# Recurrence of a hybrid encoder step: units run in pairs of head halves, their outputs placed beside the next pair

## The chip, the cores and the metric

The kernel runs on one core of a Trainium2 chip. Its time is device time in microseconds. It is given as the median of three runs; beside it stands one profiled execution, whose records are the trace that is read here. The engines are PE (TensorE, matrix products, with PEld for its weight loads), DVE (VectorE), ACT (ScalarE), POOL (GpSimd) and the DMA queues, which SP and ACT issue.

## The reference

One inference step of a two-layer encoder for two groups of requests: a prompt of 1024 tokens and eight samples of 16 tokens, 1152 tokens of width 1024. Layer 0 is RWKV-7 time mixing and a SwiGLU feed-forward part; layer 1 is chunk-band attention over one shared K and V, and a second feed-forward part. Both layers are modulated by a condition (shift, scale and gate from `silu(c) @ w_ada`). The part that the change touches is the recurrence of layer 0, over 16 heads of 64:

```python
def step(s, inp):
    r_t, w_t, k_t, v_t, a_t, b_t = inp
    sa = jnp.einsum('bhij,bhj->bhi', s, a_t)
    s = s * w_t[:, :, None, :] + sa[..., None] * b_t[:, :, None, :] + v_t[..., None] * k_t[:, :, None, :]
    y = jnp.einsum('bhij,bhj->bhi', s, r_t)
    return s, y
```

Its output y is normalised per head (mean and variance over 64), scaled, shifted, joined by a bonus term, multiplied by a gate g and projected by `rw_o`. The final states of the prompt and of the samples are outputs too.

## The kernel before

All tensors lie with features on the 128 partitions and tokens along the free dimension. The 1152 tokens are three blocks of 384 (two of the prompt, the third half prompt, half samples). Products are made in three passes over a split of each operand into a high and a low part (`split`, lines 252 to 254), which ACT and DVE make; `mm` (line 138) issues every matrix product, so that products are told apart by their tiles.

**Projections.** `proj(b)` (line 461) makes, for a block, the low-rank parts (`proj_lora`: decay, gate of a, gate g), then `proj_k`, `proj_r`, `proj_v`, each as eight tiles of features. It spills its results to memory in DRAM. The mixed operands are tiles of the tag `mix`, eight high and eight low ones for one projection; the tag has `nmix` = 17 of them. Results on their way to DRAM use tiles of the tag `e0`, four of them, through `ev` (line 453). Beside `proj_r` stand the `inverses(b)` (line 716): for each window of 128 tokens a triangular system is formed (`win_first`), solved in small blocks (`win_solve`) and put together (`win_merge`); the result is the tile TT.

**Windows.** A block has three windows of 128 tokens, and each window two halves `hf` of the heads (four feature tiles, eight heads). A unit is one window and one half. Window 8 is that of the samples. For a unit:

- `win_prep` (728) loads the spilled operands (tiles XL, BK, and UV for v), makes the local matrices by products into the bank tag G (two banks), masks them into XL and YL, and transposes BK into BKT. XL, YL and BKT have three buffers, BK has one, UV two.
- `win_run` (1015) goes through the two chunks of 64 tokens. Each `win_state` (854) has three groups of 16 products: X from UV and XL, copied to `xs` by ACT (line 877); U from `xs` and TT, copied into UV by DVE and ACT (885, 886); the state update from UV and BKT, added and scaled on DVE (910, 912); then `put_state` (940) copies the state into UV for the next chunk (942, 943). All of them use the bank tag `st`, which has two banks; `win_merge` uses it too. For window 8 both chunks run side by side, with more small products (lines 894 to 900).
- `win_y` (918) sums the outputs of a unit in the bank Y, of which there is one. It is called at the end of `win_run`.
- `win_post` (961) loads the gate and bonus (`gl`, `bv`), copies Y into the tile y (line 971, one buffer), normalises it with two products into `st` (971 to 980), applies weights and gate, and stores it to DRAM as `yg` (line 986, on ACT's queue).

The halves of one window don't depend on each other; window w+1 needs the state of window w of the same half.

**Order.** Each part is a generator that yields after a step. `windows(us)` (1031) prepares two units, then runs unit i woven with the output of unit i-1, and prepares one more unit after each run. `alternate(a, b, m, n)` (1004) takes m steps of a and n of b in turn. In `layer0a` (1088) the windows of block b-1 alternate with `proj(b)` at 5 to 4. After the last projections, when the projections' tiles have been released and the pool `tail` has taken their place, the units of windows 6 to 8 alternate at 5 to 2 with `early()`: 32 steps of the modulation (`ada_steps`, weights `in_wada`, loaded into tiles `raw`) and the output projections of blocks 0 and 1 (`outproj`, 1062). `outproj(2)` comes last; it reloads `yg` into tiles `mr` (1070), splits them into `mx` and multiplies. The tail's units are, in this order, (6,0), (6,1), (8,0), (7,0), (7,1), (8,1).

The order in which these generators issue instructions is a priority. A planner simulates the program, and each engine's own order comes from that simulation, by priority among what it takes to be ready. An engine then works through its own list in order, and each queue of DMAs too.

Of the kernel before, what the change touches and what calls it, by code (L numbers as in the profile page):

```python
# [136 lines left out]
def mm(nc, out, lhsT, rhs, start, stop):  # L137
    return nc.tensor.matmul(out, lhsT, rhs, start=start, stop=stop)  # L138


class Trunk:
# [196 lines left out]
    def proj_open(self, ctx):  # L338
        self.pp = ctx.enter_context(self.tc.tile_pool(name="proj", bufs=1, side="right", reuse_waits="tile"))
        self.rawc, self.rawtag = 1024, "raw"  # L340
        self.nraw, self.nhi, self.nlo = 3, 2, 2
        self.nmix, self.nmr = 17, 2
        pp = self.pp
        self.hb = pp.tile([128, 8, 408], F32, name="hb")

# [142 lines left out]
    def proj_r(self, b, hi, lo):  # L488

        nc = self.nc  # L490
        for f in range(8):
            W = self.wunit(self.pp, self.a["rw_r"][f])
            pz = self.bank("acc", 2)
            self.gemm(pz[:, :TB], W, hi, lo)
            kp = self.ev("ag", 2)
            self.load(kp, "kp", b, f)
            ex = self.ev("rr", 2)
            self.load(ex, "cs", b, f)
            nc.scalar.activation(ex, ex, AF.Exp, scale=-KAPPA)
            nc.vector.scalar_tensor_tensor(kp, pz[:, :TB], self.P("rk", f), kp, ALU.mult, ALU.mult)  # L500
            nc.vector.tensor_tensor(ex, ex, pz[:, :TB], ALU.mult)
            self.spill("r", b, f, ex)
            aux = self.bank("aux", 1)
            mm(nc, aux[:, :TB], self.C("bo"), kp, True, True)
            bn = self.ev("e0", 4)
            nc.scalar.activation(bn, aux[:, :TB], AF.Copy)
            self.save("bn", b, f, bn)
            yield

    def proj_lora(self, b, hi, lo):  # L510

        nc, pp = self.nc, self.pp
        split = lambda ts: tuple([self.hgroups(t)[i] for t in ts] for i in range(2))
        (hc, hp), (lc, lp) = split(hi), split(lo)

        def first(n, rows):
            pw = self.bank("acc", 2)
            W = [self.wunit(pp, dt, 8 * rows) for dt in self.lw[n]]
            for i, (h, l) in enumerate(((hc, lc), (hp, lp))):
                for k in range(8):  # L520
                    s = slice(k * rows, (k + 1) * rows)
                    self.mm3(pw[:rows, :TB], W[i][0][:, s], W[i][1][:, s], h[k], l[k], i + k == 0, i + k == 8)
            return pw

        def second(n, t, bias, spill):
            wh, wl = self.wunit(pp, self.a[n])
            for f in range(8):
                fs = slice(f * 128, (f + 1) * 128)
                pz = self.bank("acc", 2)
                mm(nc, pz[:, :TB], wh[:, fs], t, True, False)  # L530
                mm(nc, pz[:, :TB], wl[0:64, fs], t[0:64], False, True)
                sg = self.ev("e0", 4)
                ins = nc.scalar.activation(sg, pz[:, :TB], AF.Sigmoid, bias=self.P(bias, f))
                if spill == "cs":
                    nc.vector.tensor_tensor_scan(sg, rs, sg, 0.0, ALU.mult, ALU.add)
                self.save(spill, b, f, sg)
                if f % 4 == 3:
                    yield
            self.last_sg = ins

        pw = first("wa1", 128)
        yield
        tw, ta = self.ev("ag", 2, F32R), self.ev("ag", 2, F32R)
        th = self.ev("kp")
        nc.scalar.activation(th[:64], pw[:64, :TB], AF.Tanh)
        self.split(tw[0:64], tw[64:128], th[:64])
        th = self.ev("kp")
        nc.scalar.activation(th[:64], pw[64:128, :TB], AF.Copy)
        self.split(ta[0:64], ta[64:128], th[:64])
        pg = first("g1a", 128)  # L550
        yield
        th = self.ev("kp")
        h, l = self.ev("rr", 2, F32R), self.ev("rr", 2, F32R)
        nc.scalar.activation(th, pg[:, :TB], AF.Sigmoid)
        self.split(h, l, th)
        pg = first("g1b", 32)
        yield
        th = self.ev("kp")
        t = self.ev("vv", 2, F32R)
        nc.scalar.activation(th[:32], pg[:32, :TB], AF.Sigmoid)  # L560
        self.split(t[0:32], t[32:64], th[:32])
        nc.scalar.activation(t[64:96], th[:32], AF.Copy)
        rs = self.ev("rs", 1)
        nc.sync.dma_start(rs, self.a["rs"][b // 2])
        yield from second("w2", tw, "w0", "cs")
        yield from second("a2", ta, "a0", "a")
        with self.tc.issue_after(self.last_sg.ins):
            nc.scalar.preload_act_table_set("natural_log_exp_and_others")
        ah, al = self.wunit(pp, self.a["g2a"])
        raw = pp.tile([128, 1024], F32, tag="raw", name=self.nm("raw"), bufs=self.nraw)  # L570
        nc.sync.dma_start(raw[:96], self.a["g2b"])
        bh = pp.tile([128, 1024], F32R, tag="whi", name=self.nm("whi"), bufs=self.nhi)
        nc.scalar.activation(bh[:96], raw[:96], AF.Copy)
        nc.vector.tensor_tensor(bh[64:96], raw[64:96], bh[64:96], ALU.subtract)
        for f in range(8):
            fs = slice(f * 128, (f + 1) * 128)
            pz = self.bank("acc", 2)
            self.mm3(pz[:, :TB], ah[:, fs], al[:, fs], h, l, True, False)
            mm(nc, pz[:, :TB], bh[:96, fs], t[:96], False, True)
            g = self.ev("e0", 4)  # L580
            nc.scalar.activation(g, pz[:, :TB], AF.Copy)
            self.spill("g", b, f, g)
            if f % 4 == 3:
                yield

    def proj_v(self, b, hi, lo):

        nc = self.nc
        for f in range(8):
            W = self.wunit(self.pp, self.a["rw_v"][f])  # L590
            pz = self.bank("acc", 2)
            self.gemm(pz[:, :TB], W, hi, lo)
            if b in (2,):
                self.step(1)
            vv = self.ev("vv", 2)
            self.load(vv, "bn", b, f)
            v = self.ev("e0", 4)
            nc.scalar.activation(v, pz[:, :TB], AF.Copy)
            nc.vector.tensor_tensor(vv, vv, pz[:, :TB], ALU.mult)
            nc.scalar.activation(vv, vv, AF.Identity, bias=self.P("lnb", f))  # L600
            self.spill("v", b, f, vv)
            pt = self.bank("aux", 1)
            for w in range(3):
                nc.tensor.transpose(pt[:, w * 128:(w + 1) * 128], v[:, w * 128:(w + 1) * 128], self.C("ident"))
            vt = self.ev("e0", 4)
            nc.scalar.activation(vt, pt[:, :TB], AF.Copy)
            for e in range(2):
                nc.sync.dma_start(self.sv[b][:, :, e, f, :].rearrange("w p d -> p w d"),
                                  vt.rearrange("p (w e d) -> p e w d", w=3, e=2)[:, e])
            yield  # L610
# [117 lines left out]
    def win_prep(self, w, hf):  # L728

        nc = self.nc  # L730
        smp = w == 8
        b, wi = divmod(w, 3)
        fs = slice(4 * hf, 4 * hf + 4)
        R = Ctx()
# [37 lines left out]
        for e in range(2):  # L772
            nc.scalar.activation(bkt[:, :, e], pt[e].rearrange("p (c f d) -> p c (f d)", c=2, f=4), AF.Copy)
        R.xl, R.yl, R.bkt, R.TT = xl, yl, bkt, self.TT.pop((w, hf))
        uv = R.uv = self.wt("UV", [128, 2, 2, 4, 64], 2)
        for c in range(2):
            for e in range(2):
                p0 = 64 * (1 - e)
# [75 lines left out]
    def win_state(self, w, hf, c, R):  # L854

        nc = self.nc
        TT, xl, uv, bkt = R.TT, R.xl, R.uv, R.bkt
        hs = [slice(0, 64), slice(64, 128)]
        smp = w == 8
        xs = self.wt(f"xs{c if smp else hf}", [128, 4, 64], 1)  # L860
        X = self.bank("st", 2)
        if smp:
            sv = R.sv[c]
# [151 lines left out]
    def win_run(self, w, hf, R):  # L1015
        if w == 8:
            self.win_smp(hf, R)
            gens = [self.win_state(w, hf, c, R) for c in range(2)]
            while gens:
                gens = [g for g in gens if next(g, StopIteration) is not StopIteration]  # L1020
                yield
        else:
# [3 lines left out]
                yield from self.win_state(w, hf, c, R)  # L1026
            if w == 7:
                self.nc.sync.dma_start(self.o["wkv_p"][:, 4 * hf:4 * hf + 4, :], self.S[hf])
        R.Y = self.win_y(w, hf, R)

    def windows(self, us):

        us = list(us)
        n = 2
        r = []
        for u in us[:n]:
            r.append(self.win_prep(*u))
            yield
        for i in range(0, len(us) + 1, 1):
            gens = [self.win_run(*u) for u in r[i:i + 1]]  # L1040
            if i > 0:
                gens += [self.win_post(*u) for u in r[i - 1:i]]
            yield from self.woven(*gens)
            for u in us[len(r):len(r) + 1]:
                r.append(self.win_prep(*u))
                yield


    def tail_open(self, ctx):
# [809 lines left out]
```

## Time and profile before

| | us |
|---|---|
| median of three runs | 3941.44 |
| lowest, highest run | 3936.35, 3944.1 |
| profiled execution | 3918.74 |
| its span, first to last instruction | 3917.0 |
| granted TensorE clock, mean | 0.93 |
| first copy of `xs` (line 877), last issue of a `yg` store (line 986) | 417.1, 1319.0 |

Rows of stages give the busy time of each engine (the union of its instructions) and their count, then the granted clock of PE as a share of full speed, the share of time that the DMA engines were busy, and GB/s. Rows of waits give who waited (engine, tile, line), what ended the wait, and then total us, times and the longest. Rows of a timeline give start, duration, engine, line, operation, tiles (out <- in) and shape; merged rows have a count. Busy times of PE are modelled from issue to end.

### The profile page before, as it was taken

What the parts mean: (1) busy time and instruction counts of PE and PEld (TensorE: products, weight loads), DVE (VectorE), ACT (ScalarE), POOL (GpSimd) and SP (SyncE); (2) the same over time, 40 slices, a digit from 0 to 9 for tenths busy, and PEclk for the clock granted to TensorE, in tenths of its full rate; (3) what the DMA queues carried; (4) which work ended last, traced back from release to release, by engine and by line L of the source; (5) the groups of instructions that cost most, each with busy time, mean ns of one, the idle gap of its engine ahead of it and who ended that gap; (6) DMA issues with size and microseconds to landing.
All of it is one profiled execution on the core that took longest, in us unless ns stands there. A gap on an engine that the chain in (4) does not pass through costs nothing.

```text
span 3917.0 us, 72405 instructions
## 1 busy us (share of the span) xinstructions
PE 3584.4 (92%) x28662; PEld 3134.8 (80%) x28662; DVE 2282.2 (58%) x4355; ACT 1586.7 (41%) x2991; POOL 575.1 (15%) x473
## 2 busy tenths in 40 slices
PE   5888999889799789999999999898889899999999
PEld 3677778677568679999888878777777789999998
DVE  3567576664535765545456852566676765455567
ACT  3555556554213443333321253455654533333310
POOL 0000000000000244545100000000000165454000
PEclk9788889799679889999999999999999999999999
DMA  5775676577646422222655213355464422222522
GB/s 201 213 240 136 195 218 183 163 228 197 182 130 189 150 92 76 74 74 73 231 204 186 103 55 101 97 152 153 148 199 156 146 72 74 76 71 94 171 80 73
DMA packets 430211, 554.27 MB, mean 142 GB/s; under 512 B 128528, under 2 KB 297872, under 8 KB 425392
## 3 DMA queue, kind: packets, MB, share of 16 engines
q1 hardware_dynamic: 375728, 530.77, 42.9%
q10 hardware_dynamic: 54144, 18.89, 2.1%
q8 instruction: 225, 3.69, 0.4%
q14 instruction: 114, 0.93, 0.1%
HBM read 415.39 MB, written 134.12 MB: 140 GB/s over the span
## 4 chain that ended last, share of the span: by engine, by line
PE 63%; DMA 8%; DVE 6%; ACT 3%; issue 2%; SPq 1%; POOL 0%; ACTq 0%; DVEq 0%; POOLq 0%
PE S L138 31%; PE PT L138 15%; PE acc L138 8%; PE st L138 3%; PE O L138 2%; DVE h L254 1%; PE PT L1685 1%; PE Y L138 1%; PE G L138 1%; PE aux L138 1%; DMA mr<-yg 1%; ACT pts L1686 1%; DMA h<-qT 0%; DMA L<-ld 0%; DMA ld<-Aab 0%
## 5 line engine op out<-in xcount | busy, mean ns | idle before, releaser
L138 PE MATMUL S<-h,w 128*128 128x320 f32 (+1 forms) x4944 | 697.5, 299 | 19.4 <-DVE h L254 8.3
L138 PEld LDWEIGHTS S<-h,w 128*128 128x128 f32 x4944 | 672.9, 191 | 31.3 <-DVE h L254 15.3
L138 PE MATMUL acc<-mx,whi 128*128 128x384 f32 (+1 forms) x1824 | 529.4, 367 | 58.3 <-ACT whi L253 19.2
L138 PE MATMUL S<-h,wh 128*128 128x320 f32 (+1 forms) x2844 | 527.8, 337 | 11.8 <-DVE h L1055 6.7
L138 PEld LDWEIGHTS S<-h,wh 128*128 128x128 f32 x2844 | 454.0, 188 | 67.7 <-issue 13.3
L138 PEld LDWEIGHTS acc<-mx,whi 128*128 128x128 f32 (+1 forms) x1824 | 345.5, 197 | 93.2 <-ACT whi L253 21.0
L253 ACT ACTIVATE w<-rq 128x512 fp32r<-128x512 f32 x308 | 192.6, 629 | 515.7 <-PE S L138 205.4
L254 DVE TENSOR_TENSOR w<-rq,w 128x512 fp32r<-128x512 f32 x308 | 269.9, 880 | 195.3 <-ACT w L253 194.4
L138 PE MATMUL PT<-h,w 128*128 128x320 f32 (+1 forms) x2448 | 354.9, 300 | 9.9 <-ACT w L253 4.3
L138 PEld LDWEIGHTS PT<-h,w 128*128 128x128 f32 x2448 | 337.5, 192 | 13.8 <-DVE h L254 5.1
L138 PE MATMUL acc<-mx,wlo 128*128 128x384 f32 (+1 forms) x912 | 329.1, 361 | 2.9 <-DVE wlo L254 2.8
L138 PE MATMUL PT<-h,wh 128*128 128x320 f32 (+1 forms) x1428 | 287.0, 344 | 11.5 <-DVE wh L254 3.9
L1244 POOL TENSOR_TENSOR t<-t,t 128x576 f32<-128x576 f32 (+1 forms) x132 | 216.1, 1638 | 416.8 <-ACT t L1251 296.3
L138 PEld LDWEIGHTS PT<-h,wh 128*128 128x128 f32 x1428 | 233.5, 190 | 41.8 <-issue 6.1
L254 DVE TENSOR_TENSOR wlo<-raw,whi 128x1024 fp32r<-128x1024 f32 (+1 forms) x123 | 145.4, 1182 | 114.4 <-ACT whi L253 113.6
L138 PEld LDWEIGHTS acc<-mx,wlo 128*128 128x128 f32 (+1 forms) x912 | 179.3, 197 | 14.7 <-DVE wlo L254 5.2
L253 ACT ACTIVATE whi<-raw 128x1024 fp32r<-128x1024 f32 (+1 forms) x123 | 125.7, 1023 | 113.1 <-PE acc L138 81.5
L254 DVE TENSOR_TENSOR h<-h,h 128x1024 fp32r<-128x1024 f32 (+4 forms) x112 | 123.4, 1116 | 80.9 <-ACT h L253 66.2
L253 ACT ACTIVATE wh<-rq 128x512 fp32r<-128x512 f32 x124 | 74.7, 625 | 229.6 <-PE S L138 144.0
L253 ACT ACTIVATE h<-h 128x1024 fp32r<-128x1024 f32 (+4 forms) x112 | 103.2, 934 | 158.4 <-DMA h<-sd 94.3
L1244 DVE TENSOR_TENSOR t<-S,t 128x576 f32<-128x576 f32 (+1 forms) x116 | 86.5, 745 | 131.6 <-PE S L138 131.5
L1311 DVE TENSOR_TENSOR h<-h,S 128x640 f32<-128x640 f32 (+1 forms) x150 | 111.9, 751 | 79.6 <-PE S L138 79.3
(399 smaller groups left out, 5706.8 us busy)
## 6 DMA issues: line engine op xcount, KB each, us to landing
h<-in_wada SPq DMA_DIRECT2D x64, 512.0 KB, 6.3
raw<-in_wada SPq DMA_DIRECT2D x48, 512.0 KB, 4.4
rq<-in_wg SPq DMA_DIRECT2D x88, 256.0 KB, 2.6
rq<-in_wu SPq DMA_DIRECT2D x88, 256.0 KB, 2.6
rq<-in_wd SPq DMA_DIRECT2D x88, 256.0 KB, 3.0
kc<-in_ck SPq DMA_DIRECT2D x16, 1024.0 KB, 5.1
vc<-in_cv SPq DMA_DIRECT2D x16, 1024.0 KB, 5.8
sd<-t SPq DMA_DIRECT2D x88, 160.0 KB, 1.9
```

Source lines behind the costliest of these rows:

```text
L138: return nc.tensor.matmul(out, lhsT, rhs, start=start, stop=stop)
L253: self.nc.scalar.activation(hi, x, AF.Copy)
L254: self.nc.vector.tensor_tensor(lo, x, hi, ALU.subtract)
L1244: eng.tensor_tensor(out, x, y, ALU.add)
L1311: nc.vector.tensor_tensor(y, y, d, ALU.add)
L1685: nc.tensor.transpose(pt[:, j * 128:(j + 1) * 128], P[:, j * 128:(j + 1) * 128], self.C("ident"))
L1686: nc.scalar.activation(pts[:, 0:nk * 128], pt[:, 0:nk * 128], AF.Copy)
```

## The change

`windows` takes the units two at a time. Both units of a pair run woven, one step of each in turn. `win_y` is no longer part of `win_run`. After the runs of a pair, the first unit's Y is made and its output is issued to the end; then the second unit's Y is made and the first step of its output is issued; what is left of that output is woven into the runs of the next pair. The next pair is prepared after that, ahead of its runs. In the tail the pairs are (6,0) with (6,1), (8,0) with (7,0), and (7,1) with (8,1).

UV gets a third buffer. The X copies of the sample window get a tile of their own, `xsm`, in the pool of the stage, with two buffers. In the projections `mix` goes from 17 to 16 buffers and `e0` from 4 to 3.

```diff
@@ proj_open
-        self.nmix, self.nmr = 17, 2
+        self.nmix, self.nmr = 16, 2
@@ proj_r, proj_lora (twice), proj_v (twice): every use of this tag in the projections
-            bn = self.ev("e0", 4)
+            bn = self.ev("e0", 3)
@@ win_prep
-        uv = R.uv = self.wt("UV", [128, 2, 2, 4, 64], 2)
+        uv = R.uv = self.wt("UV", [128, 2, 2, 4, 64], 3)
@@ win_state
-        xs = self.wt(f"xs{c if smp else hf}", [128, 4, 64], 1)
+        xs = self.st("xsm", [128, 4, 64], 2) if smp else self.wt(f"xs{hf}", [128, 4, 64], 1)
@@ win_run
-        R.Y = self.win_y(w, hf, R)
@@ windows
-        n = 2
-        r = []
-        for u in us[:n]:
-            r.append(self.win_prep(*u))
-            yield
-        for i in range(0, len(us) + 1, 1):
-            gens = [self.win_run(*u) for u in r[i:i + 1]]
-            if i > 0:
-                gens += [self.win_post(*u) for u in r[i - 1:i]]
-            yield from self.woven(*gens)
-            for u in us[len(r):len(r) + 1]:
-                r.append(self.win_prep(*u))
-                yield
+        pairs = [us[i:i + 2] for i in range(0, len(us), 2)]
+        ends = []
+
+        def prep(i):
+            for u in pairs[i] if i < len(pairs) else []:
+                r.append(self.win_prep(*u))
+                yield
+        r = []
+        yield from prep(0)
+        for i in range(len(pairs)):
+            run, r = r, []
+            yield from self.woven(*(self.win_run(*u) for u in run), *ends)
+            ends = []
+            for u in run:
+                u[2].Y = self.win_y(*u)
+                end = self.win_post(*u)
+                if u is run[0]:
+                    for _ in end:
+                        yield
+                else:
+                    next(end)
+                    ends.append(end)
+                yield
+            yield from prep(i + 1)
+        yield from self.woven(*ends)
```

More of the change, by code (lines that the diff above doesn't have):

```diff
@@ L531, in second @@
                 mm(nc, pz[:, :TB], wl[0:64, fs], t[0:64], False, True)
-                sg = self.ev("e0", 4)
+                sg = self.ev("e0", 3)
                 ins = nc.scalar.activation(sg, pz[:, :TB], AF.Sigmoid, bias=self.P(bias, f))
@@ L579, in proj_lora @@
             mm(nc, pz[:, :TB], bh[:96, fs], t[:96], False, True)
-            g = self.ev("e0", 4)
+            g = self.ev("e0", 3)
             nc.scalar.activation(g, pz[:, :TB], AF.Copy)
@@ L596, in proj_v @@
             self.load(vv, "bn", b, f)
-            v = self.ev("e0", 4)
+            v = self.ev("e0", 3)
             nc.scalar.activation(v, pz[:, :TB], AF.Copy)
@@ L604, in proj_v @@
                 nc.tensor.transpose(pt[:, w * 128:(w + 1) * 128], v[:, w * 128:(w + 1) * 128], self.C("ident"))
-            vt = self.ev("e0", 4)
+            vt = self.ev("e0", 3)
             nc.scalar.activation(vt, pt[:, :TB], AF.Copy)
```

## The prediction, made before the result was known

> **What bounds the kernel now.** First the page: span, share of the engines, granted clock in 40 slices of 98 us. The profiled execution took 3918.74 us (its span and 1.7 us around it), 22.7 us less than the median 3941.44 of the runs shown, so a sum made on the profile is moved up by 22.7 us at the end.
>
> ```profile
> span 3917.0 us, 72405 instructions
> PE 3584.4 (92%) x28662; PEld 3134.8 (80%) x28662; DVE 2282.2 (58%) x4355; ACT 1586.7 (41%) x2991; POOL 575.1 (15%) x473
> PEclk9788889799679889999999999999999999999999
> ```
>
> PE bounds the whole. The recurrence lies between 390 and 1320 us, where the clock row has its 6s, 7s and 8s. Next the busy time by stage; each row gives length, then busy us and count of PE, PEld, DVE, ACT, POOL, then clock, DMA share and GB/s.
>
> ```profile
> 390.00:700.00 310.00, 286.12 (x2793) 233.62 (x2793) 195.90 (x413) 179.42 (x337) 3.53 (x19) 0.89 0.67 195
> 700.00:1000.00 300.00, 271.85 (x3183) 223.04 (x3182) 174.88 (x401) 144.34 (x281) 6.41 (x30) 0.87 0.68 194
> 1000.00:1080.00 80.00, 57.46 (x763) 40.82 (x764) 38.64 (x102) 19.39 (x43) 0.00 (x0) 0.57 0.66 193
> 1080.00:1180.00 100.00, 96.89 (x991) 67.81 (x991) 37.35 (x97) 19.58 (x37) 0.00 (x0) 0.73 0.46 129
> 1180.00:1320.00 140.00, 132.84 (x1148) 107.84 (x1146) 74.94 (x142) 50.02 (x85) 0.00 (x0) 0.95 0.56 174
> ```
>
> In the first two stages the windows of one token block stand beside the projections of the next, and PE is busy 92% and 91%. From 1000 to 1080 PE is idle for 22.5 us and its clock is 0.57: the projections are over, the modulation's products and the windows are left. From 1080 on PE is full again. Third, what ended PE's idle time; recurrence and outputs write the tiles xs, UV, y and st. Rows of 390 to 700, then of 700 to 1000, then of 1320 to 1420:
>
> ```profile
> PE st L138 <- ACT xs L877: 4.6, 2, 4.4
> PE st L138 <- ACT UV L886: 3.6, 2, 3.3
> PE st L138 <- ACT y L978: 2.1, 1, 2.1
> PE st L138 <- ACT y L974: 0.6, 1, 0.6
> PE st L138 <- DVE UV L885: 0.5, 1, 0.5
> ...
> PE st L138 <- ACT UV L942: 2.9, 1, 2.9
> PE st L138 <- ACT UV L886: 2.6, 1, 2.6
> PE st L138 <- ACT y L971: 1.7, 1, 1.7
> PE st L138 <- DVE UV L885: 1.2, 2, 0.7
> ...
> PE acc L138 <- ACT mx L253: 12.6, 2, 9.4
> ```
>
> Recurrence and outputs cost PE 11.4 + 8.4 = 19.8 us of waits there: the 600 us are not ruled by them. The last row is the end of the stage: the output projection of the third block waits 12.6 us for split tiles that come from the last windows' outputs.
>
> Last, the first step of the first unit, from the timeline:
>
> ```profile
> 414.59 1.12 PE L138 MATMUL st<-UV,XL 128*64 128x64 f32 x16
> 417.10 0.38 ACT L877 ACTIVATE xs<-st 128x256 f32<-128x256 f32 x1
> 418.17 0.68 PE L138 MATMUL st<-xs,TT 64*64 64x64 f32 x16
> 420.54 0.22 PE L138 MATMUL Y<-YL,UV 128*64 128x64 f32 x1
> 422.59 0.41 ACT L943 ACTIVATE UV<-S 64x256 f32<-64x256 f32 x1
> 423.11 0.69 PE L138 MATMUL st<-UV,XL 128*64 128x64 f32 x16
> ```
>
> One step of a unit takes 423.11 - 414.59 = 8.5 us, of which its three groups of 16 products fill about 1.12 + 0.68 + 0.7 = 2.5; the rest are hops between engines, filled by projection products. The Y product at 420.54 stands ahead of steps that are written before it: the planner gives each engine its own order, and the place in the program is a priority.
>
> **The change part by part.** No product, copy or load is added: a unit keeps its loads in the preparation, six groups per run, two loads and one store in its output. The order moves, and buffers change.
>
> *Fewer steps for the same work.* Counted from the code, the windows of a block take 51 steps before (2 preparations, 4 x 8, 2 x 7, 3) and 41 after (2 + 13 + 13 + 11 + 2); in the tail 53 and 43. Five of them go with four of the projections' 50, so the windows are written out beside some 32 projection steps, not 40. Units 10 and 11, now at 1000 to 1037 us, get ahead of the third block's last projection products, which then fill PE after them. Of the 22.5 idle us between 1000 and 1080 I take half, **-11** (bounds 0, since the inverses of the last windows end there too, and -22.5).
>
> *Two halves in step.* The second half's products stand in the first half's hops. Half of the 19.8 us of waits goes: **-10** (bounds 0 and -19.8).
>
> *The end.* With three pairs instead of six runs in a row the last outputs come earlier, and output projections of the first two blocks are left to cover the rest.
>
> ```profile
> L986 ACTq DMA_DIRECT2D yg<-y x18: 366/416/434, 452.4 to 1319.0; - x18
> ACT y L971: 8.4, 1
> DMA to landing us min/median/max: 2.3/4.4/9.9
> ```
>
> The last store of an output is issued at 1319.0, and the last projection's operand is reloaded from it. Of the 12.6 us wait I take **-10** (bounds -12.6, and 0 if another load is last).
>
> *Outputs in turn.* The first unit's output runs whole before the second unit's Y is begun; there is one Y bank and one y tile. So the copy of Y (line 971) waits for the store of the output before it, 4.4 us in the median; it did so once, for 8.4 us. Behind that copy on ACT stand the weight splits, for which PE waits. Nine pairs: nothing if the planner puts other work ahead, 9 x 4.4 = 39.6 us if none; the row nearest is the one wait in 18: **+3**.
>
> *Preparation right before the pair.* Two units were prepared ahead, now the next pair is prepared between two pairs; with three XL buffers its second unit waits for Y of the pair before.
>
> ```profile
> 1048.59 17.14 SPq L201 DMA_DIRECT2D raw<-in_wada  x3
> ...
> 1066.47 0.61 SPq L741 DMA_DIRECT2D BK<-sp_b  x1
> ...
> 1086.37 0.58 SPq L741 DMA_DIRECT2D BK<-sp_b  x1
> ```
>
> A preparation takes 1086.37 - 1066.47 = 19.9 us from its first BK load to the next unit's, and its loads stand on SP's queue behind weight loads that wait for a buffer (17.14 us), as the modulation's loads will behind an XL load that waits for its buffer. In the two block stages projection products cover it. In the tail there are two such turns, 39.8 us: at the idle share of 1080 to 1180 (3.1%) 1.2 us, at that of 1000 to 1080 (28%) 11.2 us. **+4**.
>
> *Fewer buffers.* The tile e0 has three for four, and the mixed rows 16 for 17. UV's third buffer and the sample states' own tile take the room and cost nothing by themselves.
>
> ```profile
> L533 ACT ACTIVATE e<-acc,par x48: 555/580/587, 102.5 to 722.7; 128x384 f32<-128x384 f32 x48
> L535 DVE TENSOR_TENSOR_SCAN e<-rs,e x24: 925/950/959, 103.5 to 706.9; 128x384 f32<-128x384 f32 x24
> DMA to landing us min/median/max: 1.8/2.8/9.1
> 107.06 0.69 PE L138 MATMUL acc<-ag,wlo 64*128 64x384 f32 x1
> 108.30 0.69 PE L138 MATMUL acc<-ag,wlo 64*128 64x384 f32 x1
> L253 ACT ACTIVATE mx<-mr 128x384 fp32r<-128x384 f32 x72 | 37.3, 518 | 36.8 <-DMA mr<-yg 26.2 <-DVE mr L427 8.7 <-PE acc L138 0.9
> ```
>
> An e0 tile lives 0.58 + 0.95 + 2.8 + 0.3 (its issue) = 4.6 us in the decay's low-rank part: 1.16 us each with four, 1.54 with three, against a pace of 108.30 - 107.06 = 1.24. That is 0.3 us for 24 tiles, at most 7.2, none where other work covers; behind an eviction that waits for its tile stand ACT's copies of the recurrence and PE's weight splits: **+3**. The seventeenth mixed tile lets one split (0.52 us) go ahead at each of some 11 changes of operand, at most 5.7: **+2**.
>
> Sum: -11 - 10 - 10 + 3 + 4 + 3 + 2 = **-19 us**, 3918.7 to 3899.7 in the profile, **3922 us** as a median.
>
> **Rivals.**
>
> *Slower: the small products lose their warm surroundings.* From 1180 to 1320 the last three units' products stand among dense projection products at clock 0.95; busy time of tiles st and Y there:
>
> ```profile
> 1180.00:1320.00 140.00, 38.95 (x438) 21.11 (x438) 12.03 (x26) 9.68 (x20) 0.95 0.56 174
> 1180.00:1320.00 140.00, 15.84 (x290) 12.78 (x290) 1.79 (x3) 0.95 0.56 174
> ```
>
> If the pairs pull all of it into the stretch before, where the clock is 0.57 to 0.73 and PE full, these 54.8 us cost 54.8 x (0.95 / 0.65 - 1) = +25 us. It decides once PE is busy without a break from 1000 on: then the idle (-11) and the hops (-10) are not won either. -10 + 25 + 12 = +27: 3968 us. For it speaks that 1080 to 1180 is 97% busy at 0.73; against it, that the chain of six runs leaves PE idle just before.
>
> *No change.* The planner already lets the halves overlap, one pair of st banks serves both, and the projections cover the hops. Then -10 and +12 are left: 3943 us. For it speaks how few of the waits are the recurrence's (19.8 of 52 idle us); this is also the case that the change doesn't do what it says.
>
> *Much faster: the clock goes with the idle time.* All bounds on the gain side, -22.5 - 19.8 - 12.6, and the 57.46 busy us of 1000 to 1080 at 0.95 in place of 0.57, -23; e0 and mixed tiles +5: -73, 3868 us. Against it speaks that at 1080 to 1180 PE has almost no idle time and still 0.73. The Trainium skill, TensorE: Matmul & The Clock Gate, section "What's actually happening", says that one idle window of some 3.4 us puts the clock to half and one busy window brings it back. By that rule filled gaps would bring this rival, and the slower one would have no price; the row of 1080 to 1180 agrees with it only in part, so it keeps a small chance.
>
> **How the numbers follow.** Forecast 0.40, much faster 0.12, no change 0.22, slower 0.26. The forecast's own range, with its terms moved by half, is 3903 to 3938. The whole range, 3868 to 3972, takes in both outer cases. About 0.2%, 8 us, is what a measurement of this kernel tells from no change; the forecast's range ends 4 us inside it, so of its 0.40 some 0.36 count as faster: faster 0.51, no difference 0.21, slower 0.28.
>
> **What would show it.** Right: in the first unit pair the copies of line 877 come in twos a few us apart; PE is idle for less than 15 us between 1000 and 1080; the wait for mx at the end is under 5 us; the last yg store is issued 20 us or more before PE runs out of the second block's output projection. Wrong: the busy share of 1000 to 1200 rises with the clock under 0.7 (slower rival); line 971 waits for yg in most pairs, or line 533 for sf stores (buffer terms too small); the stages before 1000 get longer although their waits on st shrink.

## The result, and the profile after

The changed kernel takes **3896.69 us** (median of four executions, 3882.32 to 3909.43); the kernel before took 3938.89 us beside it (four, 3922.32 to 3944.1). The ratio is **0.9906**, 95% interval [0.9884, 0.9929]: 42 us less by the medians, 37 by the ratio, where 19 were forecast. A second measurement of the same changed kernel, with other executions of the kernel before, gave 0.9898 [0.9880, 0.9917].

The profiled execution of the changed kernel, 3909.43 us, is the slowest of its four; the second measurement has a profile with a span of 3891.1 us. Both are used below, because 16 us between two profiles of one kernel are more than most steps of the prediction. The profiled execution of the kernel before, 3918.74 us, lies 20 us below its median, so that the two profiles of the changed kernel show 9.4 and 25.9 us less than it and not the whole gain. The page of the changed kernel:

```profile
span 3907.6 us, 72377 instructions
PE 3567.0 (91%) x28662; PEld 3141.2 (80%) x28662; DVE 2278.3 (58%) x4355; ACT 1578.6 (40%) x2987; POOL 571.2 (15%) x473
```

As many products as before, 28662, but 17.4 us less busy time of PE. PE's idle time (span less busy) did not fall: 332.6 us before, 340.6 now, and 3891.1 - 3541.3 = 349.8 in the second profile. The profiles of the other runs below agree: the four kernels without pairs have 3575.5 to 3586.5 us of busy and 332.6 to 357.2 of idle time, the six with pairs throughout and in step 3541.3 to 3567.8 and 340.6 to 351.3. **The gain is busy time, not filled gaps.**

Where it lies is seen by cutting the span in three, at the last transpose of the third block's v (the projections end there) and at the last product of the third block's output projection. Columns as in the rows of stages. The kernel before:

```profile
0.00:1002.00 1002.00, 855.75 (x8452) 693.46 (x8452) 591.21 (x1253) 519.49 (x968) 14.45 (x73) 0.88 0.67 196
1002.00:1377.40 375.40, 326.78 (x3067) 252.51 (x3065) 196.53 (x423) 118.11 (x223) 20.49 (x16) 0.78 0.54 164
1377.40:3917.00 2539.60, 2401.82 (x17148) 2188.79 (x17146) 1494.45 (x2679) 949.14 (x1800) 540.13 (x384) 0.97 0.36 117
```

The changed kernel:

```profile
0.00:1023.30 1023.30, 871.51 (x8968) 711.59 (x8969) 609.11 (x1295) 522.23 (x988) 14.88 (x73) 0.87 0.67 195
1023.30:1355.60 332.30, 288.47 (x2550) 230.59 (x2548) 178.13 (x381) 106.10 (x199) 19.02 (x16) 0.79 0.58 176
1355.60:3907.60 2552.00, 2406.97 (x17148) 2199.03 (x17147) 1491.04 (x2680) 950.31 (x1801) 537.32 (x384) 0.97 0.36 116
```

The changed kernel, second profile:

```profile
0.00:1022.40 1022.40, 863.71 (x8969) 703.92 (x8969) 609.37 (x1295) 522.36 (x988) 14.91 (x73) 0.88 0.67 195
1022.40:1341.50 319.10, 278.40 (x2548) 222.63 (x2547) 177.66 (x381) 106.66 (x200) 19.02 (x16) 0.81 0.61 183
1341.50:3891.10 2549.60, 2399.19 (x17148) 2190.89 (x17147) 1491.60 (x2680) 950.84 (x1801) 536.44 (x384) 0.97 0.35 116
```

Some 516 products have moved from the second part into the first. The first became 21.3 and 20.4 us longer, the second 43.1 and 56.3 us shorter, and the third, whose code is the same, 12.4 and 10.0 us longer. In the first part PE's busy time rose by 15.8 and 8.0 us, in the second it fell by 38.3 and 48.4.

Which products need less of PE's time shows first in the busy time of the tiles st and Y. In the kernel before, from 1000 to 1420 us, tile st and then tile Y:

```profile
1000.00:1180.00 180.00, 64.77 (x872) 40.63 (x872) 14.71 (x34) 13.93 (x33) 0.66 0.55 158
1180.00:1420.00 240.00, 38.95 (x438) 21.11 (x438) 12.03 (x26) 9.68 (x20) 0.87 0.50 159
```

In the changed kernel, tile st:

```profile
1000.00:1180.00 180.00, 58.71 (x908) 37.82 (x908) 14.82 (x35) 13.06 (x32) 0.68 0.56 156
1180.00:1420.00 240.00, 25.11 (x332) 13.82 (x332) 8.73 (x19) 6.85 (x14) 0.85 0.51 165
```

Busy time over count, from 1000 to 1420, is 103.7 / 1310 = 79 ns for tile st before and 83.8 / 1240 = 68 after (62 in the second profile). Tile Y went the same way, 43.6 us for 646 products to 35.9 for 581. With the block stages, 390 to 1420, tiles st and Y cost PE 315.4 us before and 289.9 and 278.4 after.

This quotient is not the duration of one product. Busy time is a union, in which products that overlap count once, and tile st holds many kinds of product. Split by kind, most of the fall of st is in two kinds, both of window 8. The rows give tiles, shapes and count, then busy us and the mean ns of one product, then idle time before them. From 390 to 1420, the kernel before:

```profile
L138 PE MATMUL st<-ssv,xm 64*32 64x64 f32 x256 | 15.3, 250 | 0.0
L138 PE MATMUL st<-UV,XL 64*64 64x64 f32 x64 | 11.7, 278 | 0.0
```

The changed kernel:

```profile
L138 PE MATMUL st<-ssv,xm 64*32 64x64 f32 x256 | 7.9, 288 | 0.0
L138 PE MATMUL st<-UV,XL 64*64 64x64 f32 x64 | 3.6, 271 | 0.0
```

These two went from 27.0 to 11.5 us, 15.5 less, where the whole of st went from 228.9 to 210.4, 18.5 less. One product is not shorter (250 and 278 ns before, 288 and 271 after). What changed is the order on PE. In the kernel before, eight of the one kind and two of the other take turns:

```profile
1132.17 0.64 PE L138 MATMUL st<-ssv,xm 64*32 64x64 f32 x8
1132.74 0.47 PE L138 MATMUL st<-UV,XL 64*64 64x64 f32 x2
1133.14 0.64 PE L138 MATMUL st<-ssv,xm 64*32 64x64 f32 x8
```

In the changed kernel up to 64 of one kind stand in a row:

```profile
1112.23 1.95 PE L138 MATMUL st<-ssv,xm 64*32 64x64 f32 x64
```

In turn, ten products take 1133.14 - 1132.17 = 0.97 us, 97 ns each; in a row, 64 take 1.95 us, 30 ns each. The granted clock is 0.50 at both places.

The stages that the prediction looked at, in the changed kernel:

```profile
390.00:700.00 310.00, 280.39 (x3126) 233.11 (x3127) 193.98 (x418) 168.84 (x324) 5.31 (x19) 0.88 0.68 195
700.00:1000.00 300.00, 274.13 (x2993) 221.86 (x2992) 187.22 (x416) 152.62 (x300) 4.83 (x30) 0.88 0.69 197
1000.00:1080.00 80.00, 69.69 (x889) 57.51 (x889) 41.33 (x106) 22.38 (x50) 0.00 (x0) 0.62 0.63 168
1080.00:1180.00 100.00, 85.62 (x927) 58.81 (x926) 36.64 (x94) 18.23 (x35) 0.00 (x0) 0.72 0.50 147
1180.00:1320.00 140.00, 128.59 (x1056) 108.40 (x1056) 79.21 (x146) 54.55 (x91) 0.00 (x0) 0.92 0.66 209
```

Idle time from 1000 to 1080 went from 22.5 to 10.3 us, and from 1080 to 1180 it rose from 3.1 to 14.4. From 390 to 1000 it is 52.0 before and 55.5 after. What ended PE's idle time in the changed kernel, rows of 390 to 700, of 700 to 1000, of 1000 to 1320, and the last of 1320 to 1420:

```profile
PE acc L138 <- DVE kk L650: 5.2, 3, 4.2
...
PE st L138 <- ACT UV L942: 2.3, 2, 1.3
...
PE aux L138 <- DVE ag L500: 5.3, 1, 5.3
PE st L138 <- ACT y L971: 1.0, 1, 1.0
...
PE G L138 <- DMA BK<-sp_k: 14.1, 4, 5.2
...
PE acc L138 <- ACT mx L253: 4.0, 2, 2.3
...
PE acc L138 <- DVE e L1070: 7.7, 2, 6.2
```

The waits on the recurrence's copies are nearly gone, and waits on BK loads have come in the tail. A pair's step in the timeline:

```profile
766.87 1.98 PE L138 MATMUL st<-UV,XL 128*64 128x64 f32 x32
...
768.04 0.38 ACT L877 ACTIVATE xs<-st 128x256 f32<-128x256 f32 x1 [0.46 <-PE st L138]
768.89 0.38 ACT L877 ACTIVATE xs<-st 128x256 f32<-128x256 f32 x1 [0.47 <-PE st L138]
...
770.77 1.15 PE L138 MATMUL st<-xs,TT 64*64 64x64 f32 x32
...
776.63 1.15 PE L138 MATMUL st<-UV,XL 128*64 128x64 f32 x32
```

In this step the groups of 16 have become groups of 32, the copies come in twos, and one step of two units takes 776.63 - 766.87 = 9.8 us, where the step of one unit in the prediction took 8.5. Groups of 32 are not the rule: of the 34 groups st<-xs,TT from 390 to 1420 us four have 32 products, and 18 still have 16.

### The profile page after: what moved, and what is told of

Same layout as the page of the kernel before. It is cut to its first block, busy times and chain, and to the rows that moved or that the text cites. A ratio compares the mean times of both kernels' runs of the same rounds, so it can differ in the third digit from the quotient of the medians.

```text
span 3907.6 us, 72377 instructions
## 1 busy us (share of the span) xinstructions
PE 3567.0 (91%) x28662; PEld 3141.2 (80%) x28662; DVE 2278.3 (58%) x4355; ACT 1578.6 (40%) x2987; POOL 571.2 (15%) x473
## 3 DMA queue, kind: packets, MB, share of 16 engines
q1 hardware_dynamic: 375728, 530.77, 43.1%
## 4 chain that ended last, share of the span: by engine, by line
PE 69%; DMA 11%; DVE 9%; ACT 4%; issue 3%; SPq 1%; ACTq 0%; POOL 0%; DVEq 0%; POOLq 0%
PE S L138 32%; PE PT L138 15%; PE acc L138 11%; PE st L138 4%; PE O L138 2%; PE G L138 1%; PE PT L1696 1%; DVE h L254 1%; PE Y L138 1%; PE aux L138 1%; DMA TT<-Z 1%; DMA sp_k<-rr 1%; DMA pa<-sp_b 1%; DMA rr<-sf_cs 1%; DVE wlo L254 1%
## 5 line engine op out<-in xcount | busy, mean ns | idle before, releaser
L138 PEld LDWEIGHTS S<-h,w 128*128 128x128 f32 x4944 | 675.1, 192 | 26.7 <-DVE h L254 14.6
```

## The experiments

No kernel leaves out or changes a part of the computation. The microseconds below are differences of medians to the kernel before, measured in the same comparison (3931.88, 3930.82 and 3932.77 us in the three of them); the ratios, which have the intervals, lead to up to 5 us more or less. The change itself stands at -42, from its own measurement.

### Which half of the change

**Buffers alone.** The kernel before with the two smaller tags.

```diff
-        self.nmix, self.nmr = 17, 2
+        self.nmix, self.nmr = 16, 2
-            bn = self.ev("e0", 4)          # every use
+            bn = self.ev("e0", 3)
```

> The kernel before with e0 in three buffers and mix in 16, nothing else. If the fewer buffers are what makes the changed kernel's projections late (its last eviction of v in the first block, where no window runs yet, comes at 326.4 us against 319.2), this one is slower than before by 5 to 20 us, with that eviction 5 to 9 us later and 10 to 20 us later in the third block. If the 7 us are the planner's order alone, it lies within 4 us of before.

Measured: 1.0024 [1.0006, 1.0041], 8 us more (9 by the ratio). The loss is there, and more than the 5 us of the prediction's sum. The first block, which has no windows beside it, shows it; the transposes of v (line 604, tile e), in the kernel before:

```profile
L604 PE MATMUL aux<-cst,e x24: 270/272/332, 283.6 to 320.0; 128*128 128x128 f32 x24
```

With the smaller tags alone:

```profile
L604 PE MATMUL aux<-cst,e x24: 270/273/474, 285.6 to 329.1; 128*128 128x128 f32 x24
```

The last transpose starts 9.1 us later, and in the changed kernel 10.9 later (330.9).

**Pairs in the tail alone, and pairs in the blocks alone.** Both forms of `windows` stand in the kernel; the single one takes a unit at a time and makes Y at the end of each run. All buffers are those of the change.

```diff
 # pairs_tail: in the blocks
-                w = self.windows([(w, hf) ...])
+                w = self.windows_single([(w, hf) ...])
 # pairs_blocks: in the tail
-        for _ in self.alternate(self.windows([...]), early(), 5, 2):
+        for _ in self.alternate(self.windows_single([...]), early(), 5, 2):
```

> All buffers of the changed kernel, units one at a time beside the projections, pairs in the tail only. Theory: the gain is made in the tail, where runs in a row leave PE with little else; then the stretch from the last eviction of v to the last residual of the output projection is 330 to 345 us long (before 376.6, changed 335.6), and the kernel is 20 to 45 us faster than before. Rival: the gain comes from the second block's windows being done earlier beside the projections; then that stretch stays over 365 us, and the kernel is no faster than before by more than 5 us.

> All buffers of the changed kernel, pairs beside the projections, units one at a time in the tail. Theory: it loses what the buffers cost and wins nothing in the tail: 0 to 20 us slower than before, with the stretch from the last v to the last residual at 365 us or more. Rival (the second block's windows end earlier, so the tail starts earlier): the stretch is 350 us or less and the kernel 10 to 30 us faster.

Measured: pairs in the tail alone 0.9964 [0.9948, 0.9979], 14 us less; pairs in the blocks alone 0.9909 [0.9878, 0.9940], 37 us less. The theory that the tail's pairs make the gain **fell**: pairs beside the projections alone give as much as the whole change, as far as the intervals can tell. The two parts, 14 and 37, come to more than the whole; within the intervals they may still add. The gain shows up in the tail all the same: its second part is 338.3 us long with pairs in the blocks alone, against 375.4 before and 332.3 with both.

**Pairs in the tail, with the buffers of before.** `mix` 17, `e0` 4, two UV; the third UV of window 8 takes the place of a tile `pa` that is free by then.

```diff
-        uv = R.uv = self.wt("UV", [128, 2, 2, 4, 64], 3)
+        uv = R.uv = self.wt("pa", [128, 2, 2, 4, 64], 1) if w == 8 else self.wt("UV", [128, 2, 2, 4, 64], 2)
```

> Units one at a time beside the projections with the buffers of before (e0 four, mix 17, UV two), pairs in the tail; the two units of the samples keep their UV in the room of pa, which only the inverses use. Theory: the tail's gain without the buffers' price, 40 to 60 us faster than before and 5 to 20 faster than the changed kernel. Rival (fewer buffers cost nothing): within 5 us of pairs_tail.

Measured: 0.9970 [0.9952, 0.9987], 14 us less, the same as with the smaller buffers, although the last transpose of v in the first block starts at 317.4 us and not at 329.6. So the loss by the buffers cannot simply be taken off every kernel that has them.

### Place in the program, or in step

The pairs take fewer steps, so that their windows are written earlier among the projections; and the two halves run in step. Two kernels have the one, one has the other.

**Singles, written earlier.** The kernel before at 6 to 4: its 51 steps then stand beside 34 projection steps, about as the 41 of the pairs do at 5 to 4.

```diff
-                for _ in self.alternate(w, self.proj(b), 5, 4):
+                for _ in self.alternate(w, self.proj(b), 6, 4):
```

> The kernel before, with six steps of the windows to four of the projections in place of five to four: 51 steps then stand beside 34 of the projections' 50, as the changed kernel's 41 do at five to four (33), before 41. Theory now: the second block's last outputs come earlier because the windows have fewer steps and so an earlier place in the program; then this one gains what the changed kernel gains without its smaller buffers: 20 to 50 us faster than before, its last store of an output of that block before 1010 us (before 1037, changed 995). Rival: the step in pairs itself brings them earlier; then it is within 10 us of before.

**Pairs at the pace of before.** The changed kernel at 4 to 4: 41 steps beside 41.

```diff
-                for _ in self.alternate(w, self.proj(b), 5, 4):
+                for _ in self.alternate(w, self.proj(b), 4, 4):
```

> The changed kernel with four steps of the windows to four of the projections: its 41 steps stand beside 41 of the projections, as before's 51 did. Theory (place in the program): most of the gain is lost, 0 to 15 us faster than before, the second block's last store at 1020 us or later. Rival (pairs in step): still 30 us or more faster than before, that store before 1005 us.

**Pairs, but not in step.** Everything of the change, only that the second unit's run follows the first's; at 7 to 4, since that takes more steps.

```diff
-            yield from self.woven(*(self.win_run(*u) for u in run), *ends)
+            yield from self.woven(self.win_run(*run[0]), *ends)
+            yield from self.win_run(*run[1])
```

> The changed kernel, but the second unit of a pair runs after the first and not in step with it, at seven to four, so that its 59 steps stand beside 34 of the projections. Theory (place in the program): within 12 us of the changed kernel, 25 to 45 us faster than before. Rival (pairs in step): the waits of PE on st come back and it is less than 15 us faster than before.

| | written as before | written earlier |
|---|---|---|
| one unit after the other | 1 | singles 0.9984 [0.9971, 0.9996]; pairs not in step 0.9971 [0.9957, 0.9985] |
| two in step | 0.9935 [0.9914, 0.9956] | 0.9906 [0.9884, 0.9929] |

In microseconds: -6 and -11 for the place, -25 for the step, -42 for both. **Being in step is the larger part**; its interval ends where those of the place alone begin. The pairs not in step have every other part of the change, and the change is 26 us faster than they are by the ratios (29 by its second measurement): about the same size by another way. This second way is not quite clean, since in the tail they stay at 5 to 2 with more steps, so that their windows are written later there.

The busy time of tiles st and Y from 390 to 1420 us goes with the step in these kernels: 315.4 us before, 305.4 and 305.0 for the place alone, 288.3 for the step alone, 289.9 and 278.4 for both. But window 8's two kinds are part of it, and they follow the tail: 27.0 us before, 23.9 for singles written earlier, 14.6 for pairs not in step, 10.7 for the step alone, 11.5 for both, and still 27.4 with pairs in the blocks alone, which gain 37 us. Without these two kinds it is 288.4, 281.5 and 290.4 us where no units are in step, and 277.6, 278.4 and 266.9 where they are: some 10 us go with the step.

What does not decide is when the second block's outputs end. The last store of an output before 1060 us, in the kernel before:

```profile
L986 ACTq DMA_DIRECT2D yg<-y x7: 377/416/434, 707.1 to 1036.9; - x7
```

With pairs in the blocks alone (0.9909):

```profile
L986 ACTq DMA_DIRECT2D yg<-y x6: 383/418/597, 806.6 to 996.6; - x6
```

With pairs not in step (0.9971):

```profile
L986 ACTq DMA_DIRECT2D yg<-y x6: 382/418/686, 815.5 to 997.2; - x6
```

With pairs at the pace of before (0.9935):

```profile
L986 ACTq DMA_DIRECT2D yg<-y x7: 378/383/426, 708.0 to 1027.0; - x7
```

Pairs not in step end as early, 997, as pairs in the blocks alone, and gain a third of it; pairs at the old pace end 30 us later and gain more than twice as much as they do. The explanation that an earlier end of the second block's windows lets the tail's chain start earlier is thus not sufficient.

### Better versions, and two more suspects

**The changed kernel with the buffers of before**: `mix` 17, `e0` 4, two UV and `pa` for window 8, as above.

> The changed kernel with the buffers of before in the projections (e0 four, mix 17) and two of UV; the samples' two units keep their UV in the room of pa. Theory: the first block's last transposes of v come at 320 us again (before 320.0, changed 330.9), and the kernel is 5 to 15 us faster than the changed one, so 45 to 55 faster than before. Rival: what the first block wins the second and third lose, since the next pair's loads into UV wait for Y: within 5 us of the changed kernel.

Measured: 0.9912 [0.9892, 0.9932], 38 us less: no faster than the change itself (0.9906 and 0.9898). The first block is back, its last transpose of v starts at 321.7 us:

```profile
L604 PE MATMUL aux<-cst,e x24: 270/273/477, 281.4 to 321.7; 128*128 128x128 f32 x24
```

So the buffers are worth 9 us in the first block here too, and the end of the program doesn't show it. Which of the other two changes of this kernel (UV with two buffers for three, the place of `pa`) eats it was not tried by itself.

**A tile of its own for window 8's local matrix.** In the kernel before, window 8's local matrix waits for a tile `Aab` and holds the G banks until then, and the tail's first preparation needs these; it was suspected that this is what the pairs set free. The tiles `shin` and `shout` share a place to make room.

```diff
-        aab = self.wt("Aab", [128, 8, 64], 2)
+        aab = self.wt("Aab8", [128, 8, 64], 1) if w == 8 else self.wt("Aab", [128, 8, 64], 2)
```

> The kernel before; only the masked matrix of the samples' window (Aab of window 8) has a buffer of its own (the two small shift tiles share one, to make room). In the trace of before both G banks are held by that window's products until its Aab can be written at 1046.7 and 1047.6 us, when the merge of window 7 has let go of its own Aab, and the first preparation of the tail stands behind them (its BKT at 1064.4; changed kernel 1020.0 and 1031.3). Theory: this hold is how the late merge makes the tail late; then the first BKT of the tail comes before 1040 us and the kernel is 10 to 30 us faster than before. Rival: the tail's units wait for the engines and not for the banks; then within 6 us of before.

> pairs_room with the same buffer for window 8's Aab. Theory: in pairs the merge is early already (Aab at 1011.6 and 1014.5 there), so less is left: 0 to 12 us faster than pairs_room. Rival (the hold costs nothing): the same as pairs_room within 5 us, and as slow where the early solve takes DVE from the projections.

Measured: 1.0014 [1.0000, 1.0028] on the kernel before, 0.9933 [0.9911, 0.9954] on the changed kernel with more room, which has 0.9912 without it. The suspicion **fell**. The edit does what it should; the copies of BKT and the first copies of xs around the start of the tail, in the kernel before:

```profile
L773 ACT ACTIVATE BKT<-G x2: 597/597/597, 1064.4 to 1066.5; 128x512 f32<-128x512 f32 x2
...
L877 ACT ACTIVATE xs<-st x2: 378/380/383, 1060.2 to 1085.4; 128x256 f32<-128x256 f32 x2
```

With the tile of its own:

```profile
L773 ACT ACTIVATE BKT<-G x6: 591/597/597, 987.7 to 1059.7; 128x512 f32<-128x512 f32 x6
...
L877 ACT ACTIVATE xs<-st x3: 384/384/384, 1069.5 to 1084.6; 128x256 f32<-128x256 f32 x3
```

The preparation comes 77 us earlier, the runs do not, and nothing is gained.

**The next pair prepared ahead of the outputs**, in the changed kernel with more room.

```diff
             ends = []
+            yield from prep(i + 1)
             for u in run:
                 u[2].Y = self.win_y(*u)
                 ...
-            yield from prep(i + 1)
```

> pairs_room with the next pair's preparation written ahead of the pair's outputs. In the changed kernel PE waited 14.1 us for BK loads between 1000 and 1320 us, four times, 0.2 us before. Theory (the preparation right before the pair costs a few us of the tail): 3 to 12 us faster than pairs_room. Rival: the preparation then holds the G banks and the outputs come later, 0 to 15 us slower than pairs_room.

Measured: 0.9955 [0.9939, 0.9971], 15 us less than before, but more than the same kernel without this edit (0.9912): by 17 us as the ratios stand, by 23 as the medians do. It costs where it was to gain. From the end of the second block's projections to that of the third's, without the edit:

```profile
666.50:1017.40 350.90, 317.11 (x3852) 262.32 (x3851) 212.71 (x471) 174.19 (x345) 7.24 (x30) 0.88 0.65 185
```

And with it:

```profile
658.50:1046.20 387.70, 345.15 (x3943) 278.18 (x3941) 214.55 (x482) 173.09 (x341) 8.36 (x30) 0.82 0.61 172
```

36.8 us longer for 91 products more, at a clock of 0.82 instead of 0.88. So a preparation right ahead of its pair is not a cost of the change but the better place. Why PE has a lower clock there was not followed further.

**The changed kernel again.**

> The changed kernel itself, on the chip of the three others: 30 to 45 us faster than before, within 6 us of what pairs_room showed.

Measured: 0.9898 [0.9880, 0.9917], 41 us less. No other version is clearly faster than it.

## Why the prediction was right and where it was not

The sign held, and the whole range (3868 to 3972 us) took the result in. The forecast's own range, 3903 to 3938, did so only at its edge: 3896.69 us lies below it, and the ratio applied to the median that the forecast was added to, 0.9906 x 3941.44 = 3904.4, just inside. That range is also not what its working gives: with all terms moved by half it runs from 3901 to 3944. The size was half of what came. The three gains were priced as idle time of PE, and PE's idle time did not fall; the gain came as busy time, for which the sum has no term. That the sign came right is in part luck. One of the signs of being wrong did appear: the first part of the span became 21.3 us longer although its waits on recurrence and outputs shrank. It was no loss, since 516 products came with it and the second part became 43.1 us shorter.

*Fewer steps for the same work (-11).* The sign that was named came true: 10.3 us of idle time from 1000 to 1080, 12.2 less. But 11.3 us of idle time appeared from 1080 to 1180, so that as a count of idle time the step won nearly nothing. The step failed in what it counted. Moving products from the second part of the span among the projections changes what they cost, and this was not in the sum. The second part lost 38.3 us of PE's busy time; 15.5 of them are window 8's two kinds, which stand there before and after, so that some 23 are left for the 516 products that moved, and these brought 15.8 to the first part. The difference is near what the place is worth by itself, 6 and 11 us in the two kernels that have it alone.

*Two halves in step (-10).* Being in step is the larger part of the gain, 25 us when it is alone; the way was not the one given. PE's waits on recurrence and outputs fell from 19.8 to 2.7 + 1.6 = 4.3 us from 390 to 1000, but other waits (kk, ag) took their place, and the idle time of these stages stayed (52.0, 55.5). What fell is the busy time of the recurrence's products, above all in the tail: some 10 us of it go with the step, and 15.5 are window 8's two kinds. For these two the trace shows how: they no longer take turns on PE. They lose part of their cost without the step too (14.6 us in pairs not in step), and pairs in the blocks alone gain 37 us with all of it (27.4). So how being in step shortens the program is shown only in part.

*The end (-10).* Right: the wait for mx fell from 12.6 to 4.0 us (3.1 in the second profile). Its sign was half right. PE runs out of the second block's output projection here, in the changed kernel:

```profile
1296.38 0.33 PE L138 MATMUL acc<-mx,whi 128*128 128x384 f32 x1
1297.46 0.44 PE L138 MATMUL acc<-mx,whi 128*128 128x384 f32 x1 [0.74 <-DVE mx L254]
```

The last store is issued 12.6 us ahead of it, not 20. What is late next is the sum at line 1070 of the changed kernel, 7.7 us; the same sum, line 1059 of the kernel before, was waited for 6.3 us there.

*Outputs in turn (+3).* The waits came as feared and cost little. Tile yg in the changed kernel:

```profile
L986 ACTq DMA_DIRECT2D yg<-y x18: 361/416/597, 452.9 to 1283.8; - x18
...
  ACT y L971: 21.9, 8
...
DMA to landing us min/median/max: 2.3/4.2/8.3
```

The copy of Y waited 8 times, 21.9 us, where it had waited once, 8.4. PE's waits for that copy are 0.2 us from 390 to 700 and 1.0 from 700 to 1000. The sign given for this being too small (line 971 waits in most pairs) appeared, and the conclusion tied to it did not follow: of these 21.9 us on ACT, 40% busy, hardly any reached PE.

*Preparation right before the pair (+4).* PE did wait 14.1 us for BK loads from 1000 to 1320, more than the upper of the two values worked out (11.2). But the other place is the worse one: ahead of the outputs the preparation costs 17 us more by the ratios.

*Fewer buffers (+3, +2).* Alone they cost 8 us, the sum's 5 being below it and the upper bounds 7.2 + 5.7 above it. The term counted e0 for the decay's 24 tiles only; the first block, 9 us late, has no windows beside it, so there it is the projections' own work that is late. Which tile's wait makes it was not singled out. In kernels with pairs the total doesn't show this loss (0.9912 with the larger tags, 0.9906 and 0.9898 with the smaller).

*Slower rival.* It didn't come, and for the reason opposite to the one priced: few products of tiles st and Y are pulled from the stretch at clock 0.95 into the slower one before it, and they need less busy time in both. From 1180 to 1320 in the changed kernel st has the 25.11 us of the row of 1180 to 1420, and Y:

```profile
1180.00:1320.00 140.00, 11.39 (x226) 9.71 (x226) 1.79 (x3) 0.92 0.66 209
```

36.5 us for 558 products, where 728 took 54.8; the clock from 1000 to 1080 rose from 0.57 to 0.62 (0.66 in the second profile).

*No change.* Refuted: copies in twos (in the first pair from its second step on), and a ratio clear of 1.

*Much faster.* Not reached. Its rule was that the clock goes with the idle time. By the Trainium skill, TensorE: Matmul & The Clock Gate, section "What's actually happening", an idle window lowers the clock and a busy one restores it. From 1080 to 1180 the idle time rose from 3.1 to 14.4 us and the clock went from 0.73 only to 0.72 (0.77 in the second profile, with 16.1 idle us): the traces of this case do not show the clock following the idle time there.

**What stays open.** Busy time of st and Y doesn't rank all runs: pairs in the blocks alone have 300.1 us of it and gain 37 us, pairs in the tail alone 293.4 and gain 14. Each is one profile, and that of pairs in the blocks alone is 17 us slower than its median, that of the kernel before 13 to 20 faster; two profiles of the changed kernel differ by 11.5 us in this sum. The mean granted clock is not separated from the change either: it was 0.934 in the changed kernel's second measurement against 0.926 in the kernel before beside it, but 0.925 to 0.930 in the first, with the same ratio. And the last part of the program, with the same code and the same 17148 products, is 12.4 and 10.0 us longer after the change; its cause was not looked for. It lasts 2545 and 2549 us in two kernels without pairs (the tile of its own, the smaller buffers), so that most of this need not come from the pairs.

## What to carry to other kernels

Where a chain of small products runs beside dense work, count what its products cost in each stretch (busy time, by tile and then by kind), not only the gaps around them: here PE's idle time over the span did not fall at all, and products of one kind in a row cost a third of what they and another kind cost in turns. Busy time over count is not the duration of a product, so look at both before saying what became cheaper. A wait that is sure to come prices nothing until it is said which engine it holds up and whether that engine sets the end. And vary place and grouping apart before saying which one paid: written earlier alone gave 6 to 11 us, in step alone 25.

## What the runs showed of the hardware that was not expected

- A PE stretch can be 97% busy at a granted clock of 0.73, and 86% busy at 0.72 (1080 to 1180 us, before and after): idle time does not tell the clock there.
- Eight products of one shape and two of another in turn took 97 ns each, 64 of the first shape in a row 30 ns each, both at a granted clock of 0.50 (window 8, tile st, before and after).
- One program's profiles differ by 16 us of span (3907.6 and 3891.1), 13 of them in the 330 us between the last projections and the last output projection (332.3 and 319.1), and its four times by 27 us (3882.32 to 3909.43). A single profile is not enough to price steps of 5 us in this kernel.
- Nine microseconds won back at 320 us (first block, more buffers) were not seen at the end of the kernel with pairs, where two other things changed with them, while nine lost there were seen in the kernel before.
